# VectorE's convolution taps accumulate in PSUM, and GpSimd takes ten taps of 31 instead of nine

## The chip, the core and the metric

One NeuronCore of one Trainium2 chip runs the whole program. The metric is the device time of one execution in microseconds. TensorE (PE), VectorE (DVE), ScalarE (ACT) and GpSimd (POOL) each work through their own instructions in order and wait for each other by semaphores; SyncE (SP) issues most of the DMAs. VectorE and ScalarE can reach SBUF and PSUM, TensorE writes to PSUM, and GpSimd works on SBUF alone in this program.

## The reference

Two layers of a token mixer with a feed-forward part, then a second block, all in float32, on 512 tokens of width 1024 and (in the first layer only) 256 context tokens. The mixer has three branches: a convolution, an mLSTM and a latent attention. The convolution branch is what the change touches:

```python
CONV_DIM = 512
CONV_K = 31
def conformer_conv(a, w_dw, b_dw, g, b, w_pw):
    val, gate = jnp.split(a, 2, axis=-1)
    h = val * jax.nn.sigmoid(gate)
    h = lax.conv_general_dilated(h, w_dw[:, None, :].astype(h.dtype), (1,), ((CONV_K // 2, CONV_K // 2),),
                                 dimension_numbers=('NWC', 'WIO', 'NWC'), feature_group_count=CONV_DIM) + b_dw
    return jax.nn.silu(layer_norm(h, g, b)) @ w_pw
```

Each of 512 features has a filter of its own with 31 taps over time; then a layer norm over the features, a SiLU and a product.

## The kernel before

Features lie on the 128 partitions, tokens along the free axis: 768 tokens (512 and 256 of the context) in layer 0, 512 in layer 1. Each float32 product is made of three matmuls on two exact parts of each factor. So each weight unit that arrives by DMA is split into `whi` (ScalarE, L421) and `wlo` (VectorE, L422: raw minus whi, both in SBUF), two units ahead of its use.

The order of the instructions on each engine is the order in which the Python code traces them. A stage has a main line, which makes TensorE's products, and a side line. Both are generators. The main line yields the time that its products should take by a nominal rate (0.96 us for a step of 128 input features with 768 tokens, 0.64 us with 512), which advances a clock; the side's next step is traced once the clock has come to it (`weave_list`, L533). A negative yield of the side is a steady pace: the next step is due that long after the last.

In the convolution stage (from L1500) the main line is: four pairs of products for the gated linear unit (GLU, `Conv.glu`, L1163), the output product of the mLSTM branch (`branch_out`, L1117, eight output tiles), then eight products of the branches' gates (`gates`, L1113). Each GLU pair gives one tile of 128 features: ScalarE makes the sigmoid `cg` (L1169) and VectorE the product `hp` (L1173), which reads PSUM and has zeros around it. The products' results lie in three PSUM tiles of two banks each (`b2`); a product that finds all three in use makes TensorE wait for their readers. Two tiles of one bank (`b1`) are for small things.

The side line is `Conv.side` (L1241). First the taps of the four tiles (L1177): VectorE begins with tap 0 and the bias (L1189) and adds the next ones up in `acc`, one instruction per tap, hp times a weight plus acc (L1192), with hp and acc in SBUF. The last nine taps of the 31 go another way: ScalarE scales `hp` by the tap's weight (L1197 the first one into `ac2`, L1201 the others into `tap`), and GpSimd adds them up in `ac2` (L1202). One such tap is traced beside every second tap of VectorE. At the end VectorE adds `ac2` to `acc` (L1205). In layer 0 the two token ranges are convolved as one row of 783 columns. `ac2` has one buffer, `acc` four. After that comes the layer norm (L1209): for each group of 128 tokens, TensorE transposes the four `acc` tiles into a `b1` tile (L1216, through L602), VectorE takes mean and variance (L1220 to L1222), GpSimd the reciprocal root (L599), VectorE normalizes (L1227); then TensorE transposes back into `b2` tiles, ScalarE applies SiLU (L1236), and the result is split (L593, L594). When the main line is over, what is left of the side is traced at once (L1509), and then comes the branch's output product (L1511).

`psum_banks` (L453) sets how the eight banks are divided. `TAP_PACE` (L181) is the side's pace per tap, for layers 0 and 1.

Of the kernel before, what the change touches and what calls it, by code (L numbers as in the profile page):

```python
# [17 lines left out]
P = 128  # L18
# [18 lines left out]
# ---------------------------------------------------------------- weight stream  # L37
def weight_plan():
    """Units of the weight stream in the order in which the kernel uses them:
    (key, array, layer, first row, row tiles, columns; -1 is a zero column)."""  # L40
# [119 lines left out]
# heads 1 to 3 of the mLSTM, and the gates of the branches (branch, output tile), in the order of  # L160
# their products: beside the mLSTM, beside the convolution, beside the attention
# [5 lines left out]
def start_cols(g):  # L167
    """shift and scale of two feature tiles."""
    return np.concatenate([np.arange(a + g * 256, a + (g + 1) * 256) for a in (0, D)])
# [11 lines left out]
TAP_PACE = (1.27, 1.35)  # L181
# [11 lines left out]
# ---------------------------------------------------------------- vectors, one column per 128 features  # L193
# [40 lines left out]
def prepare(inputs):  # L234
    """Lays the inputs out for the chip: packs, permutes and pads, nothing else."""
    f = {k: np.asarray(v) for k, v in inputs.items()}
    out = {}
# [85 lines left out]
    # second block: block-diagonal pairs of heads, transposed mixing weights  # L323
# [55 lines left out]
# ---------------------------------------------------------------- the kernel  # L379
class Weights:  # L380
    """Streams the weights: loads each unit, splits it into two exact parts."""

    def __init__(self, nc, pool, ws):
        self.nc, self.pool, self.ws = nc, pool, ws
        self.plan = weight_plan()
        self.off = np.concatenate([[0], np.cumsum([unit_width(u) * P for u in self.plan])])
        self.index = {u[0]: i for i, u in enumerate(self.plan)}
        self.raw, self.parts = {}, {}
        self.place = {}  # where the parts of a unit go, other than in the rings
        self.loaded = self.split = self.used = 16  # L390
# [44 lines left out]
def build(tc, T_, out, dbg=None, stop=None):  # L435
    """T_: name -> DRAM AP of the laid-out inputs."""
# [6 lines left out]
def _build(es, tc, nc, IN, out, dbg, stop):  # L443
# [9 lines left out]
    def psum_banks(n2, n1):  # L453
        """n2 tiles of two banks and n1 of one bank."""
        if ps_cfg:
            ps_cfg["stack"].close()
        ps_cfg.update(n2=n2, n1=n1, stack=ExitStack())
# [16 lines left out]

    psum_banks(3, 2)
# [9 lines left out]
    # ---- constants  # L485
# [30 lines left out]
    # ---- interleaving: generators trace the work step by step and yield microseconds,  # L516
    # those of the tensor engine for products, those to wait for before the next step for a Side
    clock = [0.0]

    class Side:  # L520
# [3 lines left out]
        def step(self):  # L524
# [3 lines left out]
            elif r < 0:  # a steady pace rather than a wait  # L528
# [4 lines left out]
    def weave_list(main, sides):  # L533
        """traces main; in between the steps of the sides that are due; -> what main returns."""
# [23 lines left out]
    # ---- small helpers  # L558
    def a_steps(ps, wp, n0, u, kt, segs):
        """feature-major product: stationary weight tile, tokens moving; a step for each k."""  # L560
# [12 lines left out]
    def grouped(items, sides=None):  # L573
        """several units of u at once, token group by token group, each group as soon as
        its side has made it; -> their PSUM tiles."""
# [28 lines left out]
    # ---- modulation vectors  # L604
# [5 lines left out]
    def mod_products(ps, ws, k0=0):  # L610
        """four row tiles at a time, each in columns of its own; their sums are added up later."""
# [17 lines left out]
    def mod_cols(l, nb):  # L629
        """features on partitions: modT[l][:, block, (x, ctx)]."""  # L630
# [8 lines left out]
    def mod_rows(l, nb, dst):  # L639
        """broadcast over partitions: dst[r] is [P, 512] for r in (x, ctx)."""  # L640
# [8 lines left out]
    # ---- activations of the linear layers, split in two parts  # L649
# [7 lines left out]
    def affine(l, which):  # L657
        """1 + scale and shift of layer l's mixer (0) or feed-forward part (1)."""
# [5 lines left out]
    def norm_affine(l, ln, lm, which):  # L664
        """gain and bias of normalized -> modulated input, from the norm ln of layer l."""
# [18 lines left out]
    # ---- layer 0: u from x, ctx, beside the first products  # L684
# [57 lines left out]
    # lower bounds of the forget gates: softmax and running sum over one layer, less its first  # L742
# [9 lines left out]
    # 8 softplus(-lam) = 8 max(-lam, 0) + 8 log1p(exp(-|lam|)), the latter as 2 atanh(e / (2 + e))  # L752
# [32 lines left out]
    # ---------------------------------------------------------------- mLSTM  # L785
    class MLstm:
        """heads: tiles of each head; lanes: gates as rows 0-3 forward, 32-35 backward."""
# [34 lines left out]
        def values(self, h):  # L822
            """the values of head h with tokens on partitions, and ones beside them."""
# [25 lines left out]
        def lanes(self):  # L849
# [64 lines left out]
            # -M and exp(m - M) as two parts each, broadcast later over the partitions  # L914
# [45 lines left out]
        def scan(self, h):  # L960
# [18 lines left out]
            # keys weighted for the states  # L979
# [9 lines left out]
            # states at the start of each chunk  # L989
# [22 lines left out]
            # decay matrices, transposed: sources on partitions  # L1012
# [55 lines left out]
            # norm over the head, gate  # L1068
# [26 lines left out]
    # ---------------------------------------------------------------- gated branches  # L1095
    last_act = {}

    def after_act():
        """what is traced in this context stays behind the main line on the scalar engine."""
# [5 lines left out]
    def gate(l, b, sp, n):  # L1105
        """one output tile of the gates of branch b, before the sigmoid; it waits in DRAM."""
# [10 lines left out]
    def branch_out(l, b, Y, pp, merged=None):  # L1117
        """merge += gate * (Y @ w); the partial sums wait in DRAM until the last branch (2)."""
# [32 lines left out]
    # ---------------------------------------------------------------- convolution branch  # L1151
    class Conv:
        NPOOL = (9, 9)
# [23 lines left out]
        def taps(self):  # L1177
            l, n, cp = self.l, self.n, self.cp
            for i in range(4):
# [6 lines left out]

                acc = cp.tile([P, 784], F32, tag="acc", name=nm("acc"), bufs=4)
                ac2 = cp.tile([P, 784], F32, tag="ac2", name=nm("ac2"), bufs=1)
                V.tensor_scalar(acc[:, :n], hp[:, :n], tap(0), vcol("b_dw", l, i), op0=ALU.mult, op1=ALU.add)  # L1189
                side = list(range(31 - self.NPOOL[l], 31))  # L1190
                for j, k in enumerate(range(1, 31 - self.NPOOL[l])):
                    V.scalar_tensor_tensor(acc[:, :n], hp[:, k:k + n], tap(k), acc[:, :n], op0=ALU.mult, op1=ALU.add)  # L1192
# [12 lines left out]
                V.tensor_add(acc[:, :n], acc[:, :n], ac2[:, :n])  # L1205
# [3 lines left out]
        def norm(self, Y):  # L1209
            l, cp, To = self.l, self.cp, self.To  # L1210
            tok = []
            for t in range(self.nt):
                c0 = t * P if t < 4 else 527 + (t - 4) * P
                pt = b1()
# [32 lines left out]
    # ---------------------------------------------------------------- latent attention  # L1247
# [6 lines left out]
    def latent(l, lp, tp, what, gname, seg, width, acc):  # L1254
        """bias and gain of a latent; the norm's factor is applied later, per token; acc: sum of squares."""
# [15 lines left out]
    def latent_factor(tp, acc, rc, rb, To, width):  # L1271
        """factor of the norm, with tokens on partitions (rc) and over all partitions (rb)."""
# [17 lines left out]
    def mla_inputs(l, qpool, kv_stack):  # L1290
        """queries and keys of all heads [96, tokens], values with tokens on partitions."""
        segs, To = segs_of(l), width_of(l)
        QT = [qpool.tile([P, T], F32, tag=f"Q{h}", name=nm("Q")) for h in range(8)]
        with pool(f"ckv{l}", side="right") as kp:
            with pool(f"cq{l}") as lp:
# [5 lines left out]
                def rotated_keys():  # L1301
                    """the rotated part of the keys, the same for all heads."""
# [78 lines left out]
    def attend(l, QT, KTt, vt, ap, qpool, Y):  # L1381
        """softmax attention by pairs of heads; Y takes the place of the queries."""
# [20 lines left out]
        def transposed(t, prs):  # L1403
            """keys on partitions: for each head its key tiles."""
# [48 lines left out]
    def att_fill(l, ap, g1):  # L1453
        """the products that run beside the attention: gates of its branch, modulation vectors."""
# [24 lines left out]
    def mixer(l, left, right, pre):  # L1479
        """everything up to the merged branches; -> their parts and the gains g1."""  # L1480
        with pool(f"sg{l}", side="right") as sp, pool(f"ya{l}", side="right") as ypool:
# [18 lines left out]
            with pool(f"conv{l}") as cp, pool(f"bra{l}") as pp:  # L1500
                phase(f"glu{l}")
                conv = Conv(l, cp)
# [8 lines left out]
                drain(branch_out(l, 0, conv.Y, pp))  # L1511
            if stop == f"conv{l}":
                return None
# [924 lines left out]
```

## Time and profile before

| | us |
|---|---|
| median of 3 runs | 3278.22 |
| lowest and highest run | 3275.84, 3284.81 |
| span of the profiled execution | 3279.6 |
| TensorE busy | 3169.9 (97%) |
| VectorE busy | 1944.0 (59%) |
| ScalarE busy | 1171.6 (36%) |
| GpSimd busy | 476.3 (15%) |

The profile is of one execution, and all durations here are from it. A busy TensorE means that its instructions followed each other, not that it ran at its peak. The granted clock, a share of full speed, stands beside it where a stretch is shown. An engine's idle time is given with the instruction that ended it. The convolution stage of layer 0 lies between about 320 and 560 us, that of layer 1 between about 1770 and 1950 us.

### The profile page before, as it was taken

To read this page: it belongs to the slowest core of one execution; us is meant where nothing else is said; L and a number is where in the kernel's file an instruction comes from. 1 tells how busy PE (TensorE), PEld (TensorE's weight loads), DVE (VectorE), ACT (ScalarE), POOL (GpSimd) and SP (SyncE) were. 2 spreads that over 40 slices of the span, in tenths; PEclk is the share of its full clock that TensorE was granted. 3 is DMA by queue.
4 is the path that set the end of the run, shared out by engine and by line. 5 is a ranking of instruction groups with operands and counts; after the bars stand their busy time and mean duration, and the time that the engine had idled before them with its cause. 6 is when DMAs were issued, how large, how long until landed. Compare 5 with 4: busy or idle time off the path is not lost.

```text
span 3279.6 us, 41784 instructions
## 1 busy us (share of the span) xinstructions
PE 3169.9 (97%) x16944; PEld 2594.3 (79%) x16944; DVE 1944.0 (59%) x2829; ACT 1171.6 (36%) x1650; POOL 476.3 (15%) x376
## 2 busy tenths in 40 slices
PE   8999899999999999999999889999999999999998
PEld 5889788877788888888888668677788877888887
DVE  5555995555663343356656966567454677566565
ACT  2322343344523222123423333453332356533234
POOL 0011552100011220012002341001110132000000
PEclk9999999999999999999999989999999999999999
DMA  5112145132432232232223452354432232332232
GB/s 223 50 62 96 43 156 169 64 106 94 155 120 71 87 113 87 84 90 78 74 73 109 135 161 68 101 195 140 138 109 90 85 115 71 122 103 97 95 104 71
DMA packets 103328, 344.92 MB, mean 105 GB/s; under 512 B 12448, under 2 KB 13088, under 8 KB 102112
## 3 DMA queue, kind: packets, MB, share of 16 engines
q1 hardware_dynamic: 92000, 309.44, 29.0%
q0 software_dynamic: 4128, 16.89, 1.4%
q10 hardware_dynamic: 7008, 15.93, 1.3%
q8 instruction: 133, 2.18, 0.3%
q14 instruction: 59, 0.48, 0.0%
HBM read 309.48 MB, written 32.70 MB: 104 GB/s over the span
## 4 chain that ended last, share of the span: by engine, by line
PE 41%; DVE 5%; issue 2%; DMA 1%; ACT 1%; POOL 1%; SPq 0%; POOLq 0%; ACTq 0%; DVEq 0%
PE b L566 23%; PE b L1615 4%; PE b L1617 4%; PE b L1616 4%; DVE acc L1192 2%; PE b L602 1%; PE b L1391 1%; DVE wlo L422 1%; PE b L1426 1%; PE b L614 1%; DMA bsig<-sig_dram 1%; PE b L2036 1%; DMA bo<-in_r_b_out 0%; PE b L998 0%; POOL hx L2021 0%
## 5 line engine op out<-in xcount | busy, mean ns | idle before, releaser
L566 PE MATMUL b<-uh,whi 128*128 128x512 f32 (+1 forms) x2800 | 893.7, 360 | 12.1 <-ACT whi L421 4.4
L566 PE MATMUL b<-ul,whi 128*128 128x512 f32 (+1 forms) x2800 | 871.4, 352 | 3.0 <-DVE ul L594 2.9
L566 PE MATMUL b<-uh,wlo 128*128 128x512 f32 (+1 forms) x2800 | 870.9, 351 | 1.9 <-DVE wlo L422 1.9
L422 DVE TENSOR_TENSOR wlo<-raw,whi 128x1024 fp32r<-128x1024 f32 (+1 forms) x400 | 518.6, 1298 | 591.4 <-ACT whi L421 590.9
L421 ACT CAST whi<-raw 128x1024 fp32r<-128x1024 f32 (+1 forms) x400 | 416.3, 1042 | 1048.5 <-PE b L566 563.3
L566 PEld LDWEIGHTS b<-uh,whi 128*128 128x128 f32 x2800 | 481.9, 190 | 114.5 <-issue 27.1
L566 PEld LDWEIGHTS b<-uh,wlo 128*128 128x128 f32 x2800 | 481.0, 189 | 82.4 <-issue 5.9
L566 PEld LDWEIGHTS b<-ul,whi 128*128 128x128 f32 x2800 | 481.7, 190 | 78.1 <-DVE ul L594 4.9
L1615 PE MATMUL b<-whi,fh 128*128 128x512 f32 x816 | 319.7, 392 | 0.0
L1617 PE MATMUL b<-whi,fh 128*128 128x512 f32 x816 | 319.4, 391 | 0.0
L1616 PE MATMUL b<-wlo,fh 128*128 128x512 f32 x816 | 319.0, 391 | 0.0
L1192 DVE SCALAR_TENSOR_TENSOR acc<-hp,vec,acc 128x783 f32<-128x783 f32 (+1 forms) x168 | 206.0, 1260 | 1.4
L1617 PEld LDWEIGHTS b<-whi,fh 128*128 128x128 f32 x816 | 153.3, 188 | 34.5 <-DVE fh L1783 1.2
L1615 PEld LDWEIGHTS b<-whi,fh 128*128 128x128 f32 x816 | 153.3, 188 | 32.8
L566 PE MATMUL b<-y,whi 128*128 128x512 f32 x576 | 152.7, 374 | 27.4 <-DVE hp L1173 13.6
L1616 PEld LDWEIGHTS b<-wlo,fh 128*128 128x128 f32 x816 | 153.3, 188 | 32.4
L1202 POOL TENSOR_TENSOR ac<-ac,tap 128x783 f32<-128x783 f32 (+1 forms) x64 | 132.7, 2073 | 118.4 <-ACT ac L1197 75.4
L566 PEld LDWEIGHTS b<-y,whi 128*128 128x128 f32 x576 | 100.0, 199 | 49.0 <-DVE hp L1173 14.9
L1825 DVE TENSOR_TENSOR acc<-acc,b 128x1024 f32<-128x1024 f32 x60 | 73.2, 1220 | 87.8 <-PE b L1617 87.7
L1394 DVE TENSOR_REDUCE sm<-b 128x1 f32<-128x768 f32 (+1 forms) x80 | 68.0, 850 | 95.1 <-PE b L1391 91.3
L624 POOL DMA_DIRECT2D bm<-in_b_mod x20 | 11.0, 549 | 704.6 <-DVE msb L626 576.8
L1391 PE MATMUL b<-K,Q 96*128 96x256 f32 (+1 forms) x288 | 100.4, 487 | 0.0
(487 smaller groups left out, 4131.8 us busy)
## 6 DMA issues: line engine op xcount, KB each, us to landing
raw<-in_ws SPq DMA_DIRECT2D x472, 512.0 KB, 3.6
sig_dram<-sig ACTq DMA_DIRECT2D x24, 384.0 KB, 2.3
bsig<-sig_dram SPq DMA_DIRECT2D x24, 384.0 KB, 4.0
m<-in_ws SPq DMA_DIRECT2D x16, 512.0 KB, 9.4
merge_dram<-bsig POOLq DMA_DIRECT2D x16, 384.0 KB, 3.9
old<-merge_dram SPq DMA_DIRECT2D x16, 384.0 KB, 4.8
sig_dram<-sig ACTq DMA_DIRECT2D x24, 256.0 KB, 2.0
bsig<-sig_dram SPq DMA_DIRECT2D x24, 256.0 KB, 4.4
```

Source lines behind the costliest of these rows:

```text
L421: nc.scalar.copy(hi[:, :w], raw[:, :w])
L422: nc.vector.tensor_sub(lo[:, :w], raw[:, :w], hi[:, :w].bitcast(F32))
L566: PE.matmul(ps[:, a:b], w, u[k][j][:, a:b], start=k == 0 and i == 0, stop=k == kt - 1 and i == 2)
L602: PE.transpose(o, i, ident)
L1192: V.scalar_tensor_tensor(acc[:, :n], hp[:, k:k + n], tap(k), acc[:, :n], op0=ALU.mult, op1=ALU.add)
L1202: G.tensor_add(ac2[:, :n], ac2[:, :n], t[:, :n])
L1391: PE.matmul(ps[:, a:b], QT[h][0:96, t * P:(t + 1) * P], KTt[h][0:96, k0 + a:k0 + b], start=True, stop=True)
L1394: V.reduce_max(sm[:, 0:1], ps[:, 0:nk], axis=AX.X)
L1615: PE.matmul(o, ah[:, cc], wp[0][:, k, :], start=st, stop=False)
L1616: PE.matmul(o, ah[:, cc], wp[1][:, k, :], start=False, stop=False)
L1617: PE.matmul(o, al[:, cc], wp[0][:, k, :], start=False, stop=sp)
L1825: V.tensor_add(acc[g][:, :, hsl], acc[g][:, :, hsl], pair(ps))
```

## The change

Three things. VectorE's running sum of a tile is a PSUM tile (`part`) instead of `acc`; the final add reads it and `ac2` and writes `acc`, in SBUF as before. GpSimd's way has ten taps of 31, so VectorE's has 21 with the first. And the pace of the side is 1.35 and 1.5 instead of 1.27 and 1.35.

For the running sum the banks are divided anew at the start of each convolution stage: three `b2` tiles, no `b1` tile, and one sum tile of two banks in layer 0 (two sum tiles of one bank in layer 1). The norm's first transposes, which had a `b1` tile, take the first bank of a `b2` tile. After the stage the banks are divided as before. The rest of the diff takes comments and docstrings out; it is left out here.

```diff
-TAP_PACE = (1.27, 1.35)
+TAP_PACE = (1.35, 1.5)
...
-    def psum_banks(n2, n1):
+    def psum_banks(n2, n1, sums=0):
...
-        ps_cfg.update(n2=n2, n1=n1, stack=ExitStack())
+        ps_cfg.update(n2=n2, n1=n1, sums=sums, stack=ExitStack())
...
+    def running_sum():
+        n = ps_cfg["sums"]
+        return ps_cfg["pool"].tile([P, 1024 // n], F32, tag="sum", name=nm("sum"), bufs=n)
...
     class Conv:
-        NPOOL = (9, 9)
+        NPOOL = (10, 10)
...
+                part = running_sum()[:, :n]
                 acc = cp.tile([P, 784], F32, tag="acc", name=nm("acc"), bufs=4)
                 ac2 = cp.tile([P, 784], F32, tag="ac2", name=nm("ac2"), bufs=1)
-                V.tensor_scalar(acc[:, :n], hp[:, :n], tap(0), vcol("b_dw", l, i), op0=ALU.mult, op1=ALU.add)
+                V.tensor_scalar(part, hp[:, :n], tap(0), vcol("b_dw", l, i), op0=ALU.mult, op1=ALU.add)
                 side = list(range(31 - self.NPOOL[l], 31))
                 for j, k in enumerate(range(1, 31 - self.NPOOL[l])):
-                    V.scalar_tensor_tensor(acc[:, :n], hp[:, k:k + n], tap(k), acc[:, :n], op0=ALU.mult, op1=ALU.add)
+                    V.scalar_tensor_tensor(part, hp[:, k:k + n], tap(k), part, op0=ALU.mult, op1=ALU.add)
...
-                V.tensor_add(acc[:, :n], acc[:, :n], ac2[:, :n])
+                V.tensor_add(acc[:, :n], part, ac2[:, :n])
...
-                pt = b1()
+                pt = b2()[:, 0:512]
...
                 phase(f"glu{l}")
+                psum_banks(3, 0, 1 if l == 0 else 2)
                 conv = Conv(l, cp)
...
                 drain(branch_out(l, 0, conv.Y, pp))
+                psum_banks(3, 2)
```

## Rows read from the trace of the kernel before

**Rows 1.** The page, busy time of each engine (share of the span, instructions).
```profile
PE 3169.9 (97%) x16944; PEld 2594.3 (79%) x16944; DVE 1944.0 (59%) x2829; ACT 1171.6 (36%) x1650; POOL 476.3 (15%) x376
```

**Rows 2.** Busy time by engine in three stretches; PEclk: granted clock.
```profile
core 0: us, PE busy (x) PEld busy (x) DVE busy (x) ACT busy (x) POOL busy (x), PEclk, DMA share, GB/s
440.00:460.00 20.00, 20.00 (x116) 17.71 (x117) 20.00 (x14) 10.01 (x12) 13.44 (x8) 1.00 0.52 181
1860.00:1880.00 20.00, 20.00 (x88) 16.05 (x87) 20.00 (x20) 12.46 (x19) 12.22 (x9) 1.00 0.62 202
395.00:400.00 5.00, 5.00 (x16) 4.23 (x17) 5.00 (x3) 0.51 (x1) 4.84 (x3) 0.50 0.00 0
```

**Rows 3.** TensorE's waits, 320 to 560 us: total, times, longest.
```profile
PE b L602 <- DVE acc L1205: 10.4, 1, 10.4
PE b L566 <- DVE hp L1173: 9.8, 1, 9.8
PE b L566 <- ACT cg L1169: 7.7, 1, 7.7
```

**Rows 4.** The same, 1770 to 2000 us.
```profile
PE b L602 <- DVE acc L1205: 9.2, 1, 9.2
PE b L566 <- ACT cg L1169: 4.4, 1, 4.4
PE b L566 <- DVE hp L1173: 3.8, 1, 3.8
...
PE b L566 <- DVE wlo L422: 1.9, 1, 1.9
```

**Rows 5.** Taps from 330 and 360 us (ns min/median/max); GpSimd's adds (us, busy) there.
```profile
L1192 DVE SCALAR_TENSOR_TENSOR acc<-hp,vec,acc x10: 1034/2541/2650, 336.3 to 359.3; 128x783 f32<-128x783 f32 x10
...
L1192 DVE SCALAR_TENSOR_TENSOR acc<-hp,vec,acc x18: 1026/1030/1036, 359.3 to 379.6; 128x783 f32<-128x783 f32 x18
...
331.00:360.00 29.00, 20.40 (x8) 1.00 0.12 38
360.00:381.50 21.50, 0.00 (x0) 1.00 0.15 50
```

**Rows 6.** VectorE by groups, 320 to 560 us: busy us, mean ns, idle before.
```profile
L1192 DVE SCALAR_TENSOR_TENSOR acc<-hp,vec,acc 128x783 f32<-128x783 f32 x84 | 123.4, 1501 | 0.8
L422 DVE TENSOR_TENSOR wlo<-raw,whi 128x1024 fp32r<-128x1024 f32 x22 | 33.6, 1533 | 16.5 <-ACT whi L421 16.5
L1142 DVE TENSOR_TENSOR bsig<-bsig,b 128x768 f32<-128x768 f32 x14 | 13.2, 944 | 15.9 <-ACT bsig L1125 11.9 <-PE b L566 4.0
...
L1173 DVE SCALAR_TENSOR_TENSOR hp<-b,vec,cg 128x512 f32<-128x512 f32 x4 | 3.0, 742 | 0.0
L1173 DVE SCALAR_TENSOR_TENSOR hp<-b,vec,cg 128x256 f32<-128x256 f32 x4 | 1.9, 474 | 0.0
```

**Rows 7.** The same, 1770 to 2000 us.
```profile
L1192 DVE SCALAR_TENSOR_TENSOR acc<-hp,vec,acc 128x512 f32<-128x512 f32 x84 | 82.6, 1018 | 0.6
L422 DVE TENSOR_TENSOR wlo<-raw,whi 128x1024 fp32r<-128x1024 f32 x30 | 43.0, 1432 | 13.1 <-ACT whi L421 13.1
```

**Rows 8.** All taps of the run: ns min/median/max, first and last start.
```profile
L1192 DVE SCALAR_TENSOR_TENSOR acc<-hp,vec,acc x168: 736/1023/2664, 336.3 to 1908.0; 128x783 f32<-128x783 f32 x84, 128x512 f32<-128x512 f32 x84
```

**Rows 9.** GpSimd by groups, 320 to 560 us.
```profile
L1202 POOL TENSOR_TENSOR ac<-ac,tap 128x783 f32<-128x783 f32 x32 | 80.2, 2506 | 67.3 <-ACT ac L1197 36.7 <-ACT tap L1201 28.7
L1144 POOL TENSOR_TENSOR bsig<-bsig,old 128x768 f32<-128x768 f32 x6 | 12.1, 2018 | 24.2 <-DVE bsig L1142 23.6 <-DMA old<-merge_dram 0.5
```

**Rows 10.** Timelines of TensorE, then VectorE, at layer 1's norm: start, us.
```profile
1910.50 0.47 PE L602 MATMUL b<-cst,acc 128*128 128x128 f32 x1 [9.21 <-DVE acc L1205]
...
1925.88 0.80 PE L566 MATMUL b<-y,whi 128*128 128x512 f32 x1
...
1911.50 0.69 DVE L1220 BATCH_NORM_STATS2 cst<-b 128x6 f32<-128x512 f32 x1
...
1913.28 0.81 DVE L1227 TENSOR_SCALAR cn<-b,cmv,crs 128x512 f32<-128x512 f32 x1 [0.69 <-POOL crs L599]
...
1921.78 1.53 DVE L1227 TENSOR_SCALAR cn<-b,cmv,crs 128x512 f32<-128x512 f32 x2 [0.45 <-POOL crs L599]
```

## The prediction, made before the changed kernel was run

> **What bounds the kernel now.** I began with the page: TensorE is busy for 97% of the span [rows 1], so only its idle time and its slow stretches can be won. The 40 slices show two dips, near 330 to 560 us and near 1770 to 2000 us; VectorE's taps lie there, so these are the convolution stages of layers 0 and 1. Then I took the list of waits of TensorE in each of them. In layer 0 three waits, 10.4, 9.8 and 7.7 us, are all that counts, 27.9 us [rows 3]. In layer 1 there are three more, 9.2, 4.4 and 3.8 us, and a small one on a weight split [rows 4]. Two kinds are seen. TensorE waits for `hp` or `cg` because the PSUM tiles of the gated linear unit (GLU) are read late: VectorE is far behind with taps, and ScalarE's sigmoid stands behind a scaling that waits until VectorE has read `ac2` (one buffer). And its transposes of the norm wait for the end of the last tile's taps. Both say that VectorE is late.
>
> Why it is late: in one layer-0 stretch the tap takes 2.541 us in the median, in the next 1.030 us. GpSimd adds in the first (8 adds) and has no instruction in the second [rows 5]. So a tap beside a GpSimd add costs two and a half times a free one; layer 0's mean is 1.501 us, layer 1's 1.018 [rows 6, 7]. In the same stages the VectorE instructions with only one input in SBUF (L1142, L1173) don't stretch: L1142 with 768 columns has a mean of 0.944 us, and L1173, the same operation as a tap, 0.742 for 512 [rows 6].
>
> **The change, part by part.** *The tap.* Its running sum moves to PSUM, so it has one SBUF input, as L1173 has. L1173 at 512 columns takes 0.742 us, the fastest tap with both inputs in SBUF 0.736 [rows 6, 8]: reading PSUM costs 6 ns. No row shows VectorE writing PSUM. The lower bound is the free SBUF tap as it stands (1.030). The upper bound is two passes per element, the read and the write of the same bank one after the other: L1173's two widths give (742 - 474)/256 = 1.05 ns per element and 0.206 us fixed [rows 6], so at double slope 0.206 + 783 x 2.10 ns = 1.85 us, and 1.28 for 512. I take 1.03 and 0.74, next to the only rows with this operation and PSUM. Per layer 80 taps and 4 first taps remain of 84 and 4. In layer 0 the taps fall from 123.4 to 80 x 1.03 = 82.4 us, in layer 1 from 82.6 to 59.2 us. The first tap, a tensor-scalar, costs 0.81 us at 512 columns with PSUM on one side [rows 10] and by the slope 1.09 at 783; eight of them, taken as no change, bound 3 us. The final add reads PSUM instead of SBUF: no change by the 6 ns.
>
> [...]
>
> *Does VectorE then keep up?* I followed the order that the code writes out, by its own clock, and set that clock to TensorE's true pace: 20 us hold 116 matmuls in layer 0 and 88 in layer 1 [rows 2], so a step of 6 (3) matmuls costs 1.034 (0.682) us where the code counts 0.96 (0.64). Between the first and the last `hp` of layer 0 TensorE has 48 steps = 49.6 us. VectorE has before 38 taps x 1.501 + 6 splits x 1.533 + 3 x 1.216 (`hp`) + 1 sum = 71 us: 21 us late, which is where 7.7 and 9.8 us come from after the PSUM tiles have given what slack they have. After: 35 x 1.03 + 9.2 + 3.6 + 1.0 = 50 us: in step. In the following branch product it has 23 taps, 4 splits, 8 `bsig` at 0.944 and a sum = 38 us against 33, then catches up in the gates (39 against 52). In layer 1 (taps at 0.74, splits at 1.432, `bsig` by the slope at 0.68) the same three are 35 against 33, 27 against 22, and 37 against 44. So both big waits per layer go, but not all slack is kept: behind by 5 us with about one product (4.1 or 2.7 us) of cover, I charge 2 us to layer 0 and 3 to layer 1; bounds 0 and 10 in all.
>
> *The tenth tap on GpSimd.* Per tile one scaling on ScalarE and one add. Nine adds at 2.02 (a free add, L1144) to 2.51 us [rows 9] are 18 to 23 us, in a chain of about 30 us: hidden by VectorE's own twenty taps. If that cover goes, the final add, and all weight splits queued behind it on VectorE, wait for the last add; see the rivals.
>
> *The slower pace.* `TAP_PACE` spreads fewer taps over more time: per tile 20 x 1.35 for 21 x 1.27, and 20 x 1.5 for 21 x 1.35 (both x 512/783). By the code's clock layer 0's norm begins at 140.2 instead of 136.3 of 153.6; layer 1's at 102.4 instead of 98.6, which is the end of the last gate product. So in layer 1 nothing covers the norm any more. The chain there: 1.0 us from transpose to statistics (1910.50 to 1911.50), four token tiles at 2.6 us (1911.50 to the end of the instruction at 1913.28), 2.6 us from the last of them (1923.31) to the branch's first matmul (1925.88) [rows 10]: 14.0 us. Now TensorE resumes at 1910.50 and starts the branch 15.4 us later, with 4.1 us of gate work (18 matmuls at 20/88 us) inside; after, 4.1 + 14.0 = 18.1 follow. Of the 9.2 us 2.7 are given back, so 6.5 are won. In layer 0 the last four back-transposes all lie behind the last gate: a transposing and an activation of the same kind, charged 3 us; bounds 1 and 5.
>
> *PSUM tiles.* The norm's transposes now take `b2`, which the gates use as well. A norm tile holds one for about its 2.6 us [rows 10], so the last gate and two transposes of layer 0 may wait up to 2.6 us each: charged 3, bounds 0 and 8. In layer 1 all gates are over by then. Rebuilding the banks twice per layer may let a product wait for the last reader (L1142, 0.944 us): charged 1, bounds 0 and 4.
>
> *The clock.* [...] Five waits of the six go (the tail of layer 1 stays): 11 us.
>
> *Sum.* Layer 0: -27.9 - 6.6 + 2 + 3 + 3 = -26.5. Layer 1: -8.2 (4.4 + 3.8) - 6.5 - 4.4 - 1.9 + 3 = -18.0. Banks +1. Together -43.5 on the profiled 3279.6: 3236. The median of the runs, 3278.2, lies 1.4 below the profiled execution, so 3235.
>
> **The rivals.** *More is won than I count:* VectorE keeps its lead everywhere and none of the charges come: -27.9 - 17.4 - 11 - 1.9 = -58, 3220. For it: consecutive taps start closer than they last. Against: the tail of layer 1 is in the code.
>
> *The side chain takes VectorE's place.* The tenth scaling is now issued two taps ahead of the final add, not four. If ScalarE is held in its queue, as it is by `bsig` loads, each of eight sums waits for a scaling (0.9) and an add (2.5) less one tap: 2.4 x 8 = 19 us, 3254. Against it: VectorE, with weight splits between its taps, is slower per pair of taps than one GpSimd add.
>
> *The change doesn't do what it says.* If the taps still stop beside GpSimd (`hp` stays in SBUF), only a tap per tile goes: 4 x 1.50 + 4 x 1.02 = 10 us, against the 9 to 10 us of charges: 3278. Against it stand the unstretched L1142 and L1173.
>
> *Slower.* A tap that reads and writes the same PSUM bank makes two passes: 1.85 and 1.28 us. It decides from 123.4/80 = 1.54 us (layer 0) and 82.6/80 = 1.03 (layer 1) on, where 80 such taps cost what the 84 did. At the bound they cost 80 x 1.85 - 123.4 = 25 and 80 x 1.28 - 82.6 = 20 us more, and VectorE is the bound in both stages, so the waits grow by it: 3323. No row shows such an instruction, so nothing in the trace excludes it; but TensorE's matmuls add into a bank at 20/88 = 0.23 us for 512 columns [rows 2], which suggests that a bank can be read and written in one pass.
>
> **How the numbers follow.** The forecast has 0.62, the side chain 0.17, more won 0.06, no effect 0.08 (the third rival and waits that merely move), slower 0.07. A change under 0.3%, 10 us, can't be told from none. Faster: 0.62 + 0.17 + 0.06 = 0.85; same 0.08; slower 0.07. The forecast's own bounds are 3224 (charges at their least) to 3250 (at their most); the range takes in the second rival and the charges at their worst, 3218 to 3256, and leaves out 2 in 10.
>
> **What would show it.** Taps at 1.03 and 0.74 us whether GpSimd adds or not, GpSimd's adds near 2.0 in layer 0, no wait of TensorE for `hp`, `cg` or `acc` over 3 us, a granted clock of 1.00 through the GLU and the branch product, and a TensorE gap of some 14 us around layer 1's norm. Taps at 1.5 us or more, or a long wait of the final add for GpSimd, would prove me wrong.

## The result, and the profile after

The changed kernel takes 3240.95 us in the median of four runs (3236.82 to 3243.78), against 3279.3 for the kernel before on the same chips: a ratio of 0.988, 95% interval 0.9869 to 0.9891. Its profiled execution has a span of 3237.7 us, 41.9 less than before. So it is faster, and the time is within 6 us of the forecast; but the term for the new banks was far too small and other charges were too large, and the experiments below are mostly about these. Of all executions below, three of 3470 to 4442 us ran at a mean granted clock of 0.65 to 0.85 and are left out of the times given.

Where the time went is read best from TensorE over the same work in both kernels: from the first `hp` of a convolution stage to the first product of the attention. Stretch and its length, then busy time and instructions of each engine, granted clock, share of the DMA engines and GB/s; layer 1, then layer 0. The kernel before:

```profile
1789.40:2052.00 262.60, 236.91 (x1031) 187.91 (x1030) 194.71 (x230) 100.58 (x136) 87.64 (x69) 0.95 0.37 117
334.40:687.70 353.30, 324.41 (x1833) 284.37 (x1832) 258.16 (x244) 121.73 (x144) 123.53 (x71) 0.95 0.31 104
```

The kernel after, the same two stretches of work:

```profile
1762.90:2009.50 246.60, 233.07 (x1031) 186.25 (x1030) 167.52 (x226) 103.65 (x140) 88.84 (x73) 0.97 0.38 124
333.50:659.90 326.40, 317.84 (x1832) 279.59 (x1831) 215.03 (x240) 124.89 (x148) 117.98 (x75) 0.99 0.34 112
```

Layer 0 is 26.9 us shorter (forecast 26.5): TensorE idles for 8.6 us instead of 28.9, and is busy for 6.6 us less with the same matmuls, because its granted clock hardly falls any more (0.99 in the mean against 0.95). Layer 1 is 16.0 shorter (forecast 18.0): idle 13.5 instead of 25.7, busy 3.8 less. VectorE's own busy time falls by 43.1 and 27.2 us.

What TensorE still waits for (engine and line waited for: total us, times, longest), kernel after, layer 0 (320 to 560 us):

```profile
PE b L570 <- DVE bsig L1146: 5.6, 1, 5.6
PE b L606 <- ACT cy L1241: 1.4, 1, 1.4
PE b L570 <- ACT cy L1241: 0.9, 1, 0.9
PE b L570 <- DVE cn L1232: 0.3, 1, 0.3
PE b L606 <- ACT sig L1114: 0.3, 1, 0.3
```

and layer 1 (1750 to 2000 us):

```profile
PE b L570 <- DVE bsig L1146: 7.3, 4, 4.1
PE b L606 <- DVE crs L1227: 3.5, 2, 3.0
PE b L606 <- DVE cn L1232: 1.5, 2, 0.8
PE b L606 <- ACT sig L1114: 0.6, 1, 0.6
```

Of the waits for `hp`, `cg` and `acc` in [rows 3, 4] none is left. In their place stands a new one, for `bsig`: VectorE's read of a product's PSUM tile (L1146, before L1142).

VectorE by groups after (busy us, mean ns, idle time before them), layer 0 and then layer 1:

```profile
L1197 DVE SCALAR_TENSOR_TENSOR sum<-hp,vec,sum 128x783 f32<-128x783 f32 x80 | 82.8, 1036 | 2.0
L422 DVE TENSOR_TENSOR wlo<-raw,whi 128x1024 fp32r<-128x1024 f32 x24 | 36.6, 1527 | 29.8 <-ACT whi L421 29.8
L1194 DVE TENSOR_SCALAR sum<-hp,vec 128x783 f32<-128x783 f32 x4 | 4.4, 1096 | 0.1
...
L1197 DVE SCALAR_TENSOR_TENSOR sum<-hp,vec,sum 128x512 f32<-128x512 f32 x80 | 56.7, 747 | 0.5
L422 DVE TENSOR_TENSOR wlo<-raw,whi 128x1024 fp32r<-128x1024 f32 x30 | 43.0, 1435 | 29.7 <-ACT whi L421 29.6
```

The taps take 1.036 and 0.747 us (forecast 1.03 and 0.74), and they no longer care about GpSimd. The 80 taps of layer 0 (ns least, median, most), with GpSimd busy for 17.93 of the first 27 us with nine adds:

```profile
L1197 DVE SCALAR_TENSOR_TENSOR sum<-hp,vec,sum x80: 1020/1037/1041, 335.8 to 461.0; 128x783 f32<-128x783 f32 x80
...
333.00:360.00 27.00, 17.93 (x9) 1.00 0.18 59
```

In [rows 5] the median beside the adds was 2.541 us. GpSimd gains too, since the two hold each other up:

```profile
L1207 POOL TENSOR_TENSOR ac<-ac,tap 128x783 f32<-128x783 f32 x36 | 74.2, 2061 | 48.5 <-ACT tap L1206 41.0 <-ACT ac L1202 5.4
```

2.06 us per add instead of 2.51 [rows 9], so nine adds per tile cost less than eight did. And where TensorE crawled at a clock of 0.50 with 16 matmuls in 5 us [rows 2], 31 now pass:

```profile
395.00:400.00 5.00, 5.00 (x31) 4.41 (x30) 4.93 (x6) 1.90 (x2) 0.54 (x1) 1.00 1.00 361
```

### The profile page after: what moved, and what is told of

Same layout as the page of the kernel before. It is cut to its first block, busy times and chain, and to the rows that moved or that the text cites. A ratio compares the mean times of both kernels' runs of the same rounds, so it can differ in the third digit from the quotient of the medians.

```text
span 3237.7 us, 41803 instructions
## 1 busy us (share of the span) xinstructions
PE 3159.7 (98%) x16944; PEld 2587.8 (80%) x16944; DVE 1872.9 (58%) x2821; ACT 1178.1 (36%) x1658; POOL 472.3 (15%) x384
## 4 chain that ended last, share of the span: by engine, by line
PE 42%; DVE 3%; issue 2%; DMA 2%; ACT 1%; POOL 1%; SPq 0%; POOLq 0%; ACTq 0%; DVEq 0%
PE b L570 23%; PE b L1622 4%; PE b L1624 4%; PE b L1623 4%; PE b L1396 1%; PE b L606 1%; DVE wlo L422 1%; PE b L1431 1%; DMA bsig<-sig_dram 1%; PE b L618 1%; PE b L2043 1%; DVE sum L1197 1%; DMA raw<-in_ws 0%; POOL ac L1207 0%; DMA g<-in_r_ln_g 0%
## 5 line engine op out<-in xcount | busy, mean ns | idle before, releaser
L422 DVE TENSOR_TENSOR wlo<-raw,whi 128x1024 fp32r<-128x1024 f32 (+1 forms) x400 | 516.6, 1292 | 621.5 <-ACT whi L421 618.1
L570 PE MATMUL b<-y,whi 128*128 128x512 f32 (+1 forms) x576 | 145.1, 359 | 2.3 <-DVE bsig L1146 1.1
L1197 DVE SCALAR_TENSOR_TENSOR sum<-hp,vec,sum 128x783 f32<-128x783 f32 (+1 forms) x160 | 139.5, 891 | 2.5
```

Of the source, the lines that this page charges most:

```text
L422: nc.vector.tensor_sub(lo[:, :w], raw[:, :w], hi[:, :w].bitcast(F32))
L570: PE.matmul(ps[:, a:b], w, u[k][j][:, a:b], start=k == 0 and i == 0, stop=k == kt - 1 and i == 2)
L1197: V.scalar_tensor_tensor(part, hp[:, k:k + n], tap(k), part, op0=ALU.mult, op1=ALU.add)
```

## The experiments

**Which part carries the gain.** The change has two parts: the sum in PSUM, and a tenth tap on GpSimd with its slower pace. Each was run alone. The sum in PSUM alone is the kernel after with

```
-        NPOOL = (10, 10)
+        NPOOL = (9, 9)
...
-TAP_PACE = (1.35, 1.5)
+TAP_PACE = (1.27, 1.35)
```

> The running sum in PSUM with its new banks, but nine taps on GpSimd and the old pace. Theory (the taps' second SBUF input was what stopped them beside GpSimd): taps of 1.03 us in layer 0 and 0.75 in layer 1; 22 taps per tile on VectorE put it some 3 us behind in the gated linear unit and 4 us more in the branch product; layer 1's norm is covered again by 3.8 us of gate work. 3235 to 3250 us, within 8 us of the changed kernel. Rival (the tenth tap carries the gain): over 3262 us.

Measured: 3239.25 us (3233.88 to 3242.01), ratio 0.988 (0.9865 to 0.9894), the same as the whole change. The opposite edit in the kernel before, ten taps on GpSimd and the new pace, with the sum left in SBUF:

> The kernel before with ten taps on GpSimd and the new pace; the running sum stays in SBUF. Theory: the taps still stop beside GpSimd, and there are four adds more per layer to stop beside, each some 1.5 us in layer 0 and 0.9 us in layer 1, against four taps less of 1.03 and 0.74 us. So VectorE gains nothing: 3272 to 3288 us, the long waits of TensorE for hp, cg and acc stay, some 45 us. Rival (the tenth tap and the pace carry the gain): under 3265 us.

Measured: 3279.71 us, ratio 1.0008 (0.9998 to 1.0017). Its taps, layer 0 and layer 1:

```profile
L1192 DVE SCALAR_TENSOR_TENSOR acc<-hp,vec,acc 128x783 f32<-128x783 f32 x80 | 123.8, 1582 | 0.8
...
L1192 DVE SCALAR_TENSOR_TENSOR acc<-hp,vec,acc 128x512 f32<-128x512 f32 x80 | 85.0, 1098 | 0.6
```

There are four taps fewer per layer, and they cost as much in all as the 84 did (123.4 and 82.6 us, [rows 6, 7]): the tap that went to GpSimd is paid for by the adds that hold up the others. TensorE's long waits stay as well, if not all in the same places: 14.1 us for `hp` in layer 0, 9.8 for `hp` and 6.5 for `acc` in layer 1. So PSUM carries the whole gain, and moving work to GpSimd is worth nothing while the taps still stop beside it.

**What in GpSimd's adds stops the tap.** The kernel before, with each GpSimd add left out and two memsets in its place, so that GpSimd writes beside the taps and reads nothing (GpSimd's taps are therefore missing from the sum):

```
-                            G.tensor_add(ac2[:, :n], ac2[:, :n], t[:, :n])
+                            G.memset(ac2[:, :n], 0.0)
+                            G.memset(t[:, :n], 0.0)
```

> The kernel before, taps in SBUF, but each of GpSimd's 64 adds is left out and two memsets of the same width (of ac2 and of the tap) stand in its place, so GpSimd is as busy, writes SBUF and reads nothing; eight taps of 31 are missing from the output. Theory (a tap with two SBUF inputs stops while a GpSimd instruction reads SBUF): no tap over 1.1 us in layer 0 or 0.8 in layer 1, though GpSimd works beside it; TensorE's long waits for hp, cg and acc go, 3228 to 3245 us. Rival (any GpSimd instruction in SBUF stops it, or its writes): tap means stay over 1.3 and 0.9 us, and the time over 3262.

Measured: 3213.18 us, ratio 0.98 (0.9781 to 0.982), under every expectation. The taps, with two SBUF inputs as before, and GpSimd's busy time beside them (17 instructions in 27 us):

```profile
L1192 DVE SCALAR_TENSOR_TENSOR acc<-hp,vec,acc x21: 1024/1034/1036, 333.9 to 358.0; 128x783 f32<-128x783 f32 x21
...
333.00:360.00 27.00, 12.55 (x17) 1.00 0.18 59
```

1.034 us beside memsets, where they took 2.541 beside adds. GpSimd is less busy here (two memsets of some 0.77 us for an add of 2.5), but it is busy for half of the stretch and not one tap of 21 stretches; of all 168 taps of the run none takes more than 1.039 us. So it is not GpSimd's writing, nor its being at work, that stops the tap; its reading from SBUF is what is left. The kernel after shows it from the other side: there the tap has one SBUF input, GpSimd's adds read SBUF beside it for 17.93 of 27 us, and no tap of layer 0 takes more than 1.041 us.

Counting SBUF inputs does not cover every instruction, though. The first tap of a tile has one SBUF input and writes SBUF in the kernel before (ns least, median, most):

```profile
L1189 DVE TENSOR_SCALAR acc<-hp,vec x8: 541/685/2194, 335.6 to 1871.3; 128x783 f32<-128x783 f32 x4, 128x512 f32<-128x512 f32 x4
```

The five that meet no GpSimd add take 0.54 to 0.69 us, the three that do 1.50 to 2.19. L1142, with one input in SBUF and one in PSUM and its output in SBUF, takes 0.94 us beside an add as without one. So the prediction's remark that instructions with one SBUF input don't stretch holds for the two that it names, not for this one.

Why this run is so much faster than the kernel after is told in part by two things. It has the old division of PSUM, whose worth is measured next. And the weight splits (L422, both inputs in SBUF) are free of the adds too:

```profile
L422 DVE TENSOR_TENSOR wlo<-raw,whi 128x1024 fp32r<-128x1024 f32 x26 | 34.1, 1311 | 32.6 <-ACT whi L421 32.6
```

1.311 us each in layer 0, against 1.527 in the kernel after. The change has freed the taps, not the splits.

**The new wait for `bsig`.** The change divides PSUM anew ahead of the convolution stage and back at its end, and the forecast charged 1 us for that. Two runs price it. First the new division and the norm's tiles alone: the kernel after with the sum back in SBUF, nine taps, the old pace.

```
-                part = running_sum()[:, :n]
...
+                part = acc[:, :n]
```

> The new banks alone: divided anew at the start and the end of the convolution stage, the norm's transposes in the larger tiles, but the running sum in SBUF, nine taps on GpSimd, the old pace. Theory: taps as in the kernel before (means 1.50 and 1.02 us), the long waits stay, and the second division adds waits of some 5 and 4 us with their slow clock: 8 to 14 us slower than before. Rival (the banks cost nothing): within 3 us of the kernel before.

Measured: 3288.32 us, ratio 1.0032 (1.002 to 1.0043): 10 us slower than before, a small but real cost. Its waits in layer 0:

```profile
PE b L570 <- DVE hp L1177: 11.0, 1, 11.0
PE b L606 <- DVE acc L1210: 10.4, 1, 10.4
PE b L570 <- DVE bsig L1146: 7.9, 2, 6.4
PE b L570 <- ACT cg L1173: 7.7, 1, 7.7
```

The three waits of before are all there again [rows 3], and `bsig` has come on top. In layer 1 this run shows only 0.6 us on `bsig`, inside the branch product and not ahead of the attention, where 4 were expected; that half is a miss, and why stays open. It is no accident of this one run: over the five runs with this late division the wait ahead of the attention is 5.2 to 6.4 us in layer 0, but in layer 1 it is none in two (this one and the sum in PSUM alone), 4.1 and 4.3 in two, and 8.8 in one.

Then the kernel after, with the second division made before the last branch product instead of behind it:

```
-                drain(branch_out(l, 0, conv.Y, pp))
                 psum_banks(3, 2)
+                drain(branch_out(l, 0, conv.Y, pp))
```

> The changed kernel, with the second division of the banks ahead of the branch's output product and not behind it. Theory: TensorE's waits of 5.6 and 4.1 us for bsig in front of the latent attention come from the new division, whose first tile lies where the branch's late product still waits for its reader; ahead of the branch product the only tiles in use are the back-transposes', whose readers the product needs anyhow. Both waits go below 1 us, and with the slow clock behind them 10 to 13 us are won on the changed kernel: ratio to it 0.996 to 0.997, some 3228 to 3232 us. Rival (the late loads of bsig are the bound, and TensorE waits for them wherever the banks are divided): 0 to 3 us.

Measured: 3229.47 us (3225.23 to 3230.24), ratio 0.9849 (0.9835 to 0.9864): 11 us better than the kernel after. Its waits in layer 0, then in layer 1:

```profile
PE b L570 <- ACT cy L1241: 2.6, 1, 2.6
PE b L606 <- ACT cy L1241: 1.4, 1, 1.4
...
PE b L606 <- DVE crs L1227: 3.2, 2, 2.5
PE b L570 <- DVE bsig L1146: 2.1, 1, 2.1
```

The 5.6 us of layer 0 and the longest of layer 1 (4.1) are gone; the 2.1 that are left stand ahead of the first gate product, as in the kernel after. The earlier division has a small price of its own: the branch product waits 2.6 us for `cy` where it waited 0.9. What happens in the kernel after is seen in the timelines of ScalarE, VectorE and TensorE at the end of layer 0's branch product (start, duration, what ended the idle time before it):

```profile
524.94 0.84 ACT L1129 ACTIVATE bsig<-bsig 128x768 f32<-128x768 f32 x1 [8.58 <-DMA bsig<-sig_dram]
...
527.89 1.81 DVE L1146 TENSOR_TENSOR bsig<-bsig,b 128x768 f32<-128x768 f32 x2
...
529.75 1.00 PE L570 MATMUL b<-uh,whi 128*128 128x512 f32 x2 [5.58 <-DVE bsig L1146]
```

The reader of the last branch tiles, L1146, needs `bsig`, which is reloaded from memory; ScalarE sits 8.6 us until that load lands. The kernel before had it too, in the timelines of ScalarE and VectorE at the same place:

```profile
562.63 0.85 ACT L1125 ACTIVATE bsig<-bsig 128x768 f32<-128x768 f32 x1 [8.25 <-DMA bsig<-sig_dram]
...
565.59 1.81 DVE L1142 TENSOR_TENSOR bsig<-bsig,b 128x768 f32<-128x768 f32 x2
```

There TensorE did not wait for it: by the code the next product takes the third tile of the same division, which is free. Behind a new division the first product of the attention's inputs takes banks of tiles whose last reader is this late one. With the division moved one product ahead, the late read falls on tiles that are not wanted yet. The clock falls a little with the wait as well: 22 matmuls in the 5 us after it, at 0.73, where 116 in 20 us at 1.00 make 29 [rows 2].

```profile
530.00:535.00 5.00, 5.00 (x22) 4.33 (x23) 1.82 (x1) 0.00 (x0) 4.38 (x5) 0.73 0.74 243
```

The first of the two divisions costs a little too: in the kernel after the first product of layer 1's convolution stage waits 1.1 us for the last reader of a gate (`sig`), where the kernel before has no wait.

**Was the slower pace a cost?** The forecast charged it 3 us in layer 0 and 2.7 in layer 1. The kernel after with the old pace:

```
-TAP_PACE = (1.35, 1.5)
+TAP_PACE = (1.27, 1.35)
```

> The changed kernel with the old pace (1.27 and 1.35). By the code's clock layer 1's norm begins 6.4 us ahead of the end of the last gate product (at it in the changed kernel) and layer 0's back-transposes are covered too; VectorE must make 38 taps instead of 35 in the gated linear unit, 3 us behind. Theory (the slower pace costs about what it saves): within 6 us of the changed kernel, 3232 to 3245. Rival (the pace was needed: waits for hp and bsig come back): over 3248.

Measured: ratio 0.9908 (0.9888 to 0.9928), 3244.97 to 3249.51 us: some 6 us slower than the kernel after, between the theory and its rival. The waits of layer 0, then of layer 1:

```profile
PE b L606 <- DVE acc L1210: 5.7, 1, 5.7
PE b L570 <- DVE bsig L1146: 5.2, 1, 5.2
...
PE b L570 <- DVE bsig L1146: 12.1, 4, 8.8
PE b L606 <- DVE acc L1210: 7.0, 1, 7.0
```

The same edit on top of the earlier division, to see it without the `bsig` wait:

> The earlier second division of the banks (run c_banks_earlier) together with the old pace. Theory: the waits in front of the latent attention stay away, and the norm is covered by gate products, against some taps more in the stage's first part: 3222 to 3231 us, at or a little under c_banks_earlier. Rival (VectorE falls behind again): over 3233.

Measured: 3236.23 us (3235.65 to 3239.27), ratio 0.9872 (0.9858 to 0.9887). That is 7 us slower than the same kernel with the slower pace, and their runs don't overlap; its waits for `acc` are 6.0 and 7.0 us. So ten taps at the old pace are 6 to 7 us slower.

But that is not the pace that the forecast compared with. Fewer taps at the same pace make a shorter tile: 20 x 1.27 = 25.4 by the code's clock in layer 0, where the kernel before had 21 x 1.27 = 26.7 and the kernel after has 20 x 1.35 = 27.0. In layer 1 it is 20 x 1.35 = 27.0 against 21 x 1.35 = 28.4 before and 20 x 1.5 = 30.0 after (all x 512/783). The tiles of the kernel before are kept in the run with the sum in PSUM alone, which has nine taps and the old pace. It took 3239.25 us against 3240.95 for the kernel after, and its waits for `acc`, layer 0 and layer 1, are these:

```profile
PE b L606 <- DVE acc L1210: 2.4, 1, 2.4
PE b L606 <- DVE acc L1210: 2.3, 1, 2.3
```

So a tile shorter than that of the kernel before costs some 7 us, and between its length, with one tap more on VectorE, and the longer one there is no difference that can be told. Ten taps at its length were not run. Why the shorter tile is late is seen in part on VectorE in the kernel after, ahead of layer 1's norm:

```profile
1857.99 2.11 DVE L422 TENSOR_TENSOR wlo<-raw,whi 128x1024 fp32r<-128x1024 f32 x1 [3.17 <-ACT whi L421]
...
1865.49 0.69 DVE L1210 TENSOR_TENSOR acc<-sum,ac 128x512 f32<-128x512 f32 x1
```

TensorE's first transpose starts at 1866.07, 0.6 us after the final add began. VectorE was just in time, though it is idle at times in this stage: its taps queue behind weight splits that wait for ScalarE's `whi` (5.5 us between the first `hp` and this add; most of the 29.6 in the row of the result falls behind it) and behind reads that wait for `bsig` (4.7). In layer 1 at the old pace these are 4.2 and 4.1 us, ahead of a final add that TensorE waits 7.0 us for. That the waits for `acc` would go without them is argued, not shown; VectorE's load counts too, as the next runs show.

**GpSimd's chain of adds as the next bound.** With the earlier division, twelve taps of 31 on GpSimd, at a pace that keeps VectorE's time per tile:

```
-        NPOOL = (10, 10)
+        NPOOL = (12, 12)
...
-                    if j % 2 == 0 and side:
+                    if j % 3 < 2 and side:
...
-TAP_PACE = (1.35, 1.5)
+TAP_PACE = (1.5, 1.667)
```

> c_banks_earlier with twelve taps of 31 on GpSimd (traced beside two of every three of VectorE's taps) and a pace that keeps a tile's length (1.5 and 1.667). GpSimd has 11 adds of 2.06 us per tile, 22.7 of some 28 us. Theory (VectorE is still the late one, GpSimd has room): VectorE has 8 taps less per layer; the waits of 2 to 3 us that are left go, 3 to 6 us under c_banks_earlier, 3223 to 3227. Rival (the side chain of ScalarE and GpSimd takes VectorE's place): the final adds wait for GpSimd, TensorE gets long waits for acc or hp again, over 3232.

Measured: 3225.76 us (3223.13 to 3228.37), ratio 0.9837 (0.9822 to 0.9852). The adds, and the final sum that would have to wait for them, layer 0:

```profile
L1207 POOL TENSOR_TENSOR ac<-ac,tap 128x783 f32<-128x783 f32 x44 | 90.2, 2050 | 39.7 <-ACT tap L1206 33.1 <-ACT ac L1202 4.2
...
L1210 DVE TENSOR_TENSOR acc<-sum,ac 128x783 f32<-128x783 f32 x4 | 3.9, 971 | 4.3 <-POOL ac L1207 4.1
```

Four final adds wait 4.1 us in all, and TensorE for none of them; in layer 1 it is 3.9 us, and again TensorE waits for none. The same with the pace (1.43, 1.55):

> The same with a faster pace (1.43 and 1.55), by which layer 0's norm lies behind gate products altogether and layer 1's begins 3.8 us ahead of their end. Theory: with the taps that it gave away VectorE holds this pace, and the cover is worth 3 to 6 us more than i_twelve_taps, 3218 to 3225. Rival (GpSimd and ScalarE can't hold it): waits for acc of some 5 us as in e_old_pace, 3228 or more.

Measured: 3221.43 to 3226.49 us, ratio 0.9827 (0.9808 to 0.9847), not to be told from the run before. Both beat the kernel before by 1.6 to 1.7% and the kernel after by some 15 us; against ten taps with the earlier division the 4 us lie inside overlapping intervals, so that step is not shown to be worth anything. At the faster pace layer 0's tile is 18 x 1.43 = 25.7 long, nearly as short as the 25.4 above, and TensorE has no wait for `acc` there, where ten taps had 5.7 and 6.0 us; in layer 1 it waits 2.1.

**The distance between taps.** In layer 0 the kernel after starts most of its taps further apart than the kernel before, though each is as long. By the code's tiles a sum of 783 columns lies across two PSUM banks, one of 512 in one. To see whether that is it, layer 1's sum was put across two banks too:

```
-                part = running_sum()[:, :n]
+                o = 0 if l == 0 else 256
+                part = running_sum()[:, o:o + n]
...
-                psum_banks(3, 0, 1 if l == 0 else 2)
+                psum_banks(3, 0, 1)
```

> The changed kernel, but layer 1's running sum lies across two PSUM banks (columns 256 to 767 of a tile of two banks). In the changed kernel taps that follow each other start 1.07 us apart in layer 0 (783 columns, two banks; 0.945 with the sum in SBUF) and 0.66 in layer 1 (512 columns, one bank; 0.66 in SBUF). Theory (the crossing of a bank makes the next dependent tap wait longer): layer 1's spacing grows by about 0.1, to 0.74 to 0.80 us. Rival (the width or the stage makes it): it stays at 0.66.

One execution: 3241.09 us. Runs of taps with nothing between them: layer 0 of the kernel after, layer 1 of it, and layer 1 with the sum across two banks (its own line numbers).

```profile
343.45 6.39 DVE L1197 SCALAR_TENSOR_TENSOR sum<-hp,vec,sum 128x783 f32<-128x783 f32 x6
...
1839.05 7.99 DVE L1197 SCALAR_TENSOR_TENSOR sum<-hp,vec,sum 128x512 f32<-128x512 f32 x12
```

```profile
1844.35 3.92 DVE L1198 SCALAR_TENSOR_TENSOR sum<-hp,vec,sum 128x512 f32<-128x512 f32 x5
```

(6.39 - 1.03)/5 = 1.07 us, (7.99 - 0.74)/11 = 0.66, and (3.92 - 0.75)/4 = 0.79: with the sum across two banks a tap starts 0.13 us later than in the second row, as the theory had it, and TensorE's waits show a new one of 3.7 us for `acc` in layer 1.

All the same it is not shown that the crossing is the cause. The edit also gives layer 1 one sum tile where it had two. And the longer distances stand where no sum crosses a bank: in the kernel before, with the sum in SBUF, in the first tile of layer 0 and at the end of its last; and in the kernel after in the first tile of layer 1, whose sum lies in one bank.

```profile
492.26 5.31 DVE L1192 SCALAR_TENSOR_TENSOR acc<-hp,vec,acc 128x783 f32<-128x783 f32 x5
```

```profile
1764.50 3.92 DVE L1197 SCALAR_TENSOR_TENSOR sum<-hp,vec,sum 128x512 f32<-128x512 f32 x5
```

(5.31 - 1.03)/4 = 1.07 and (3.92 - 0.75)/4 = 0.79, the same two numbers.

## Why the prediction was right, and where it was not

**Right, and shown.** *The tap.* 1.036 and 0.747 us for a forecast 1.03 and 0.74; the upper bound of two passes (1.85 and 1.28) is out, and with it the rival *slower*. The one neighbour that the price rested on, L1173 with its input in PSUM [rows 6], was the right one, for writing too. The first tap: 1.096 for 1.09 by slope, against a mean of 1.059 in layer 0 before, so no change as taken; but that mean was of three of 0.67 to 0.69 and one of 2.19. *The cause.* With one SBUF input fewer the tap is free beside GpSimd's reads, shown from both ends: by the change (1.041 us at most in layer 0), and by taking the reads away instead (1.039 at most). The rival *doesn't do what it says* falls with that. *GpSimd's adds* at 2.06 for 2.02 to 2.51, and the rival *side chain* falls, even at twelve taps. *The clock.* Busy time of TensorE falls by 6.6 us in layer 0 (forecast 6.6) and 3.8 in layer 1 (4.4). The forecast's 11 us are five times 2.2, by [rows 2] an estimate: 5 us at 0.50 hold 16 matmuls, where 116 in 20 us make 29. That each wait costs as much no run shows. The 5 us behind each of the five in the kernel before, three in layer 0 and two in layer 1, are these:

```profile
394.70:399.70 5.00, 4.98 (x15) 4.30 (x16) 5.00 (x3) 0.81 (x1) 4.84 (x3) 0.50 0.00 0
411.60:416.60 5.00, 5.00 (x15) 4.31 (x16) 5.00 (x6) 0.00 (x0) 0.64 (x1) 0.50 0.24 84
498.70:503.70 5.00, 4.99 (x20) 4.37 (x21) 4.15 (x7) 1.28 (x2) 0.57 (x1) 0.57 0.48 165
1828.50:1833.50 5.00, 4.98 (x12) 3.80 (x12) 5.00 (x4) 2.02 (x3) 4.76 (x4) 0.50 0.32 107
1837.80:1842.80 5.00, 4.97 (x15) 3.98 (x16) 5.00 (x7) 0.00 (x0) 1.12 (x3) 0.68 0.21 64
```

Against 29 matmuls in 5 us in layer 0 and 22 in layer 1 [rows 2] that is an estimated 6.4 and 3.9 us.

The fastest tap of 512 columns takes 0.735 us with its sum in PSUM, and 0.736 with it in SBUF [rows 8]. So at its fastest this instruction costs the same in both places, to 1 ns.

**Mis-sized: the banks.** The term "banks +1", bounds 0 and 4, was 5.6 + 4.1 = 9.7 us of waits at the second division, worth 11 us of time when it is moved, and 1.1 at the first. The step priced the last reader by its own duration, 0.944 us, and did not ask what the reader waits for. The answer stood in [rows 6]: L1142 has 11.9 us of idle time before it, put down to ScalarE's `bsig`.

**Too large: three charges.** *The slower pace*, 3 and 2.7 us of cover lost at the norm. The kind of cost was right and its size about half. In layer 0 the waits for `cy` come to 2.3 us, and the kernel before had this one:

```profile
PE b L566 <- ACT cy L1236: 0.6, 1, 0.6
```

In layer 1 the tail from the transposes to the branch product is 12.7 us (1866.07 to 1878.80) for a forecast of 14.0, so with the 4.1 us of gate work some 1.4 are given back of the 9.2 and not 2.7. The step also priced the lost cover alone, as if the tiles of the kernel before could be kept for nothing; the run that keeps them (the sum in PSUM alone) waits 2.4 and 2.3 us for `acc` and takes the same time. *The norm's tiles in `b2`* were charged 3 us in layer 0; the waits there that could be of that kind come to 0.6 us (`cn` and `sig`), and there are 0.6 for `sig` in layer 1, where none was expected. *VectorE's lag behind TensorE* was charged 5; there is no wait of that kind in layer 0, and one of 2.1 us in layer 1 (the first gate product, for `bsig`, at 1819.66).

These charges were some 7 us too large together, and the banks some 10 us too small. That the two nearly cancel is luck, and it is why the sum came out as near as it did: layer 0 to 0.4 us, layer 1 to 2. The forecast of each layer was better than its parts.

**The rival *more is won* (3220)** was not reached by the change, but most of it was there: with the division one product earlier 3229, with twelve taps 3226.

**What stays open.** Why the late division makes layer 1 wait for `bsig` in some runs and not in others; what sets the distance between taps; and what of the run without GpSimd's reads (3213) is the splits, what the shorter work of GpSimd. Freeing the splits from the adds was not tried.

## What to carry to other kernels

Where VectorE works beside GpSimd, look in its groups for one operation with two durations (here 2.541 and 1.030 us, [rows 5]); if the long one has both inputs in SBUF and GpSimd adds beside it, put the running sum into PSUM (here 1.036 us) before you move work from one engine to the other. Here a tile whose place was given anew waited for the old tile's last reader, and the price was when that reader could start, not how long it took (5.6 us for a reader of 0.95): divide where the last reads are long done. And an engine with slack in the sum of its busy times (VectorE, 59% before) can still be late at one point, if its queue holds an instruction that waits for another engine (5.5 us for `whi` and 4.7 for `bsig` in layer 1): look at its idle time ahead of that point before you give it less time.

## What the runs showed of the hardware beyond that

Taps that follow each other with nothing between them start 1.07 or 0.945 us apart with 783 columns, and 0.79 or 0.66 with 512, though they last 1.03 and 0.75 us in either case. With the sum in PSUM across two banks it is the longer distance in every tile; with the sum in SBUF (6.70 us for 7 taps, so 0.945) or in one bank it is the shorter one in most places and the longer one in some.

```profile
367.11 6.70 DVE L1192 SCALAR_TENSOR_TENSOR acc<-hp,vec,acc 128x783 f32<-128x783 f32 x7
```

An instruction that doesn't read the sum starts 0.94 to 0.95 us after a tap in layer 0 of the kernel after, if it need not wait for another engine. Over 80 taps the longer distance is at most 80 x 0.125 = 10 us of VectorE, an estimate, hidden in part; what decides between the two no run here shows.
